# The down projection of a two-layer encoder in plain and block groups, with outputs added onto the residual in DRAM

## The chip, the cores and the metric

The kernel runs on one core of a Trainium2 chip. The core has five engines with instruction streams of their own: TensorE (PE, matrix products into PSUM, with weight loads, PEld, running beside them), VectorE (DVE), ScalarE (ACT), GpSimd (POOL) and SyncE (SP), and 16 DMA engines behind queues. Here SP's queue carries the loads and POOL's queue the stores. The metric is the time on the device in microseconds (us); a smaller one is better.

## The reference, cut to what matters

The model has two layers over 1040 columns (16 learned meta columns and 1024 frames) of width 1024. The change concerns the second half of a layer, `conv_ffn`:

```python
def conv_ffn(x, w_up, conv_w, conv_b, w_down):
    h = x @ w_up
    ...
    u, g = jnp.split(hc, 2, axis=-1)
    return (jax.nn.silu(g) * u) @ w_down
...
for i in range(DEPTH):
    ...
    h = h + jnp.concatenate([o_gla, o_fox], axis=-1) @ w_out[i]
    h = h + conv_ffn(rms_norm(h, ffn_norm[i]), w_up[i], conv_w[i], conv_b[i], w_down[i])
return rms_norm(h, final_norm)[:, N_META:]
```

All is in fp32. The gated width is 2816 = 22 tiles of 128, the output width 8 tiles of 128. The last `@ w_down`, with the addition onto h, is the down projection.

## The kernel before, in words

Activations lie transposed: a tile is 128 features on the partitions by up to 1040 columns. A product of fp32 numbers is made from three matmuls (`mm3`, lines 217 to 219): each operand is split into a rounded part `hi` and a rest `lo`, and hi*hi, lo*hi and hi*lo are added in PSUM. A split is a copy on ScalarE (the cast to `hi`) and a subtraction on VectorE (`lo`): lines 184 and 186 for plain weights, 1019 and 1020 for weights of blocks, 331 and 332 for activations.

A layer runs through attention, the output projection, the up projection, and the down projection. During the output projection the residual h goes to DRAM (`hm`, line 1102, stores on POOL's queue). The up projection (`ffn_up`) works on 2 x 2 blocks: of a pair of output tiles (u and g), two halves of the inner dimension and two halves of the columns, seven block products are made instead of eight, on sums and differences of the blocks (weights: lines 980 to 1021, with `S1 = A21 + A22` made by an accumulating DMA for the first few tiles at line 996; results: copies out of PSUM by ScalarE at line 1189, additions by VectorE at 1188). Each of the 22 gated tiles is stored to DRAM (`actd`).

The down projection is the product of 22 gated tiles with a weight for 8 output tiles. `load_act` loads a gated tile from `actd` on SP's queue and splits it. `FGROUPS` cuts the 22 tiles into groups of 5, 5, 5, 4 and 3. For each of the first four groups and each output tile m, `dense3` runs the matmuls of the group over column chunks, 400, 384 and 256 wide in layer 0 and 512 and 512 in layer 1 (where the meta columns are no longer needed), with the weights of the next output tile loaded ahead (`stream`, line 205); VectorE adds the PSUM result onto h[m] on chip (line 1259), h having been loaded from `hm` as the stage begins (line 1373). The PSUM pool of this stage has eight banks of 512 numbers. The last group, tiles 19 to 21, is computed by `down_last` chunk by chunk over all eight outputs, and feeds the next layer's norm or the final one.

The order of the instructions on TensorE is that of the program text (`manual_schedule`); on VectorE, ScalarE, POOL and SP a scheduler sets the order when the kernel is built, and a queue keeps its order from then on: an instruction that waits holds up all behind it on its queue. Tiles live in a pool of equal slots on chip (`Slots`, 33 of them, with some added by stage); `get` takes a free slot, and a writer of a reused slot waits for the readers of what was there, DMAs among them.

The three central lines of the accumulation before:

```python
def ev(ps, c0, n):
    h = hT[m][:, c0:c0 + n]
    nc.vector.tensor_tensor(out=h, in0=ps, in1=h, op=ALU.add)
```

## Time and profile before

| What | Number |
|---|---|
| Median of 3 runs | 2629.63 us (2625.71 to 2631.41) |
| The profiled execution, its own time | 2631.03 us |
| Its span | 2629.3 us |
| TensorE busy | 2526.3 us, 96% of the span |
| VectorE busy | 1751.8 us, 67% |
| ScalarE busy | 1241.9 us, 47% |
| GpSimd busy | 402.9 us, 15% |
| Layer 0, groups 5, 5, 5, 4 of the down projection | 1062.30 to 1279.97 us |
| Layer 1, the same | 2365.49 to 2577.00 us |

How to read the profile's rows: a busy time is followed by its number of instructions (x...). In a row of a table by windows the columns are the window, its length, the busy time of each engine, then the clock granted to TensorE (1.00 is full), the DMA engines' busy share and GB/s. A row of a group of instructions has line, engine, operation, out<-in with shapes and count; behind the bar the busy time in us and the mean of one in ns; behind the second bar the idle time of the engine just before them and what ended it. A row with a time in front is a single instruction: start, duration, engine, line, and in brackets the idle time before it. A row of DMAs has the size of one and the median us from issue to landing.

### The profile page before, as it was taken

Reading aid. Unit: us, or ns where it says so; the run is one execution under the profiler, and the core shown is the slowest. Engines: PE = TensorE matmul, PEld = TensorE weight load, DVE = VectorE, ACT = ScalarE, POOL = GpSimd, SP = SyncE. Lnnn points to the kernel's source line nnn. Section 1 sums busy time; section 2 is a strip of 40 time slices with the busy share of each in tenths; the row PEclk is TensorE's granted clock in tenths of the full one; section 3 lists DMA queues with packets and bytes.
Section 4 is the critical chain, followed back from the end, with each engine's and each line's share of the span. In section 5 each row is a group of like instructions: output and inputs, shape, how many; then the busy total and the mean of one; then the engine's idle time right before and its main releaser. Section 6 shows DMA issues by size and latency. Waiting matters only on the chain.

```text
span 2629.3 us, 46309 instructions
## 1 busy us (share of the span) xinstructions
PE 2526.3 (96%) x18102; PEld 2407.3 (92%) x18102; DVE 1751.8 (67%) x3514; ACT 1241.9 (47%) x2677; POOL 402.9 (15%) x566
## 2 busy tenths in 40 slices
PE   8999999899999999999999999998999999999997
PEld 7988898898999999999999888888899999998886
DVE  7655766759877777643665665666698677776335
ACT  6345665635544445321443565665464444453112
POOL 4033333310000000000201333332100000000002
PEclk9999999999999999999999999999999999999999
DMA  3222123342322223522311222142523222245222
GB/s 124 67 83 71 44 86 122 105 145 89 105 77 83 80 81 100 209 90 59 106 52 66 75 73 74 56 133 92 164 73 113 79 79 74 84 154 179 62 57 75
DMA packets 117355, 245.96 MB, mean 94 GB/s; under 512 B 14752, under 2 KB 36512, under 8 KB 117136
## 3 DMA queue, kind: packets, MB, share of 16 engines
q1 hardware_dynamic: 97440, 184.89, 22.4%
q0 software_dynamic: 17824, 55.80, 6.2%
q8 instruction: 142, 2.33, 0.3%
q10 hardware_dynamic: 1872, 2.31, 0.2%
q14 instruction: 77, 0.63, 0.1%
HBM read 179.26 MB, written 50.91 MB: 88 GB/s over the span
## 4 chain that ended last, share of the span: by engine, by line
PE 76%; DVE 12%; issue 4%; ACT 4%; DMA 2%; POOL 1%; SPq 0%; DVEq 0%; POOLq 0%; ACTq 0%
PE mm L217 12%; PE mm L218 12%; PE mm L219 12%; PE up L217 9%; PE up L219 9%; PE up L218 9%; PE av L707 2%; PE tr L689 2%; DVE S L656 2%; PE wo L217 1%; PE wo L218 1%; PE wo L219 1%; DVE PT L332 1%; DVE x L1044 1%; DMA cb<-cd 1%
## 5 line engine op out<-in xcount | busy, mean ns | idle before, releaser
L217 PE MATMUL up<-x,hi 128*128 128x260 f32 (+1 forms) x2464 | 698.9, 284 | 2.3 <-ACT x L1043 1.6
L219 PE MATMUL up<-x,hi 128*128 128x260 f32 (+1 forms) x2464 | 697.8, 283 | 1.9 <-DVE x L1044 1.8
L218 PE MATMUL up<-x,lo 128*128 128x260 f32 (+1 forms) x2464 | 697.5, 283 | 0.8 <-DVE lo L1020 0.8
L219 PEld LDWEIGHTS up<-x,hi 128*128 128x128 f32 x2464 | 466.5, 189 | 2.9 <-DVE x L1044 2.9
L217 PEld LDWEIGHTS up<-x,hi 128*128 128x128 f32 x2464 | 465.9, 189 | 3.5 <-ACT x L1043 2.2
L218 PEld LDWEIGHTS up<-x,lo 128*128 128x128 f32 x2464 | 466.3, 189 | 1.0 <-DVE lo L1020 1.0
L217 PE MATMUL mm<-xh,hi 128*128 128x348 f32 (+4 forms) x1056 | 365.2, 346 | 0.0
L218 PE MATMUL mm<-xh,lo 128*128 128x348 f32 (+4 forms) x1056 | 340.9, 323 | 0.0
L219 PE MATMUL mm<-xl,hi 128*128 128x348 f32 (+4 forms) x1056 | 340.7, 323 | 0.0
L1020 DVE TENSOR_TENSOR lo<-raw,hi 128x512 fp32r<-128x512 f32 x308 | 210.1, 686 | 140.2 <-ACT hi L1019 140.2
L184 ACT CAST hi<-raw 128x512 fp32r<-128x512 f32 (+1 forms) x264 | 143.1, 544 | 334.0 <-PE mm L219 238.1
L218 PE MATMUL mm<-ah,lo 128*128 128x400 f32 (+1 forms) x760 | 266.5, 351 | 0.9 <-DVE lo L186 0.9
L219 PE MATMUL mm<-al,hi 128*128 128x400 f32 (+1 forms) x760 | 265.4, 349 | 0.0
L217 PE MATMUL mm<-ah,hi 128*128 128x400 f32 (+1 forms) x760 | 265.4, 349 | 0.0
L1019 ACT CAST hi<-raw 128x512 fp32r<-128x512 f32 x308 | 190.3, 621 | 113.8 <-PE up L219 87.2
L186 DVE TENSOR_TENSOR lo<-raw,hi 128x512 fp32r<-128x512 f32 (+1 forms) x196 | 110.8, 569 | 175.3 <-ACT hi L184 171.6
L217 PEld LDWEIGHTS mm<-xh,hi 128*128 128x128 f32 x1056 | 201.0, 190 | 6.0 <-issue 5.3
L218 PEld LDWEIGHTS mm<-xh,lo 128*128 128x128 f32 x1056 | 200.9, 190 | 0.4 <-issue 0.3
L219 PEld LDWEIGHTS mm<-xl,hi 128*128 128x128 f32 x1056 | 199.8, 189 | 0.4 <-issue 0.3
L668 ACT ACTIVATE P<-S,m 116x460 f32<-116x460 f32 (+2 forms) x224 | 125.1, 562 | 76.2 <-DVE m L656 72.1
L332 DVE TENSOR_TENSOR PT<-tr,PT 116x464 fp32r<-116x464 f32 (+3 forms) x240 | 122.1, 516 | 57.5 <-ACT PT L331 55.9
L218 PEld LDWEIGHTS mm<-ah,lo 128*128 128x128 f32 x760 | 142.8, 188 | 14.6 <-DVE lo L186 1.5
(248 smaller groups left out, 5106.5 us busy)
## 6 DMA issues: line engine op xcount, KB each, us to landing
raw<-in_wm_dram SPq DMA_DIRECT2D x338, 256.0 KB, 2.7
raw<-in_wd_dram SPq DMA_DIRECT2D x64, 256.0 KB, 2.7
actd<-cv POOLq DMA_DIRECT2D x22, 520.0 KB, 3.0
st<-actd SPq DMA_DIRECT2D x22, 520.0 KB, 4.6
actd<-cv POOLq DMA_DIRECT2D x22, 512.0 KB, 2.9
st<-actd SPq DMA_DIRECT2D x22, 512.0 KB, 4.9
cb<-cd SPq DMA_DIRECT2D x16, 520.0 KB, 4.2
kA<-kA SPq DMA_DIRECT2D x24, 260.0 KB, 3.8
```

Of the source, the lines that this page charges most:

```text
L184: nc.scalar.copy(hi[:, :n, :], raw[:, :n, :])
L186: eng.tensor_tensor(out=lo[:, :n, :], in0=raw[:, :n, :], in1=hi[:, :n, :].bitcast(F32), op=ALU.subtract)
L217: nc.tensor.matmul(ps, wh, xh[:, c0:c0 + n], start=first, stop=False, skip_group_check=more)
L218: nc.tensor.matmul(ps, wl, xh[:, c0:c0 + n], start=False, stop=False, skip_group_check=more)
L219: nc.tensor.matmul(ps, wh, xl[:, c0:c0 + n], start=False, stop=last, skip_group_check=more)
L332: nc.vector.tensor_tensor(out=lo, in0=src, in1=hi.bitcast(F32), op=ALU.subtract)
L656: nc.vector.tensor_tensor_reduce(out=S[:rows, :n], in0=S[:rows, :n], in1=cb[:rows, c0:k1], scale=1.0, scalar=(BIG if ci == 0 else m[:rows, ...
L668: nc.scalar.activation(P[:rows, :n], S[:rows, :n], AF.Exp, scale=-1.0, bias=m[:rows, nch - 1:nch], accum_out=(den if nch == 1 else d3[:row ...
L689: nc.tensor.transpose(tr[:w, j, :rows], P[:rows, o:o + w], id_)
L707: nc.tensor.matmul(av[:, a:width], w.rearrange("p a b -> p (a b)"), x, start=(t == 0 and i == 0), stop=(t == last and i == 1))
L1019: nc.scalar.copy(hi[:], src[:])
L1020: nc.vector.tensor_tensor(out=lo[:], in0=src[:], in1=hi[:].bitcast(F32), op=ALU.subtract)
```

## The change

The 19 tiles that were in groups of 5, 5, 5 and 4 are now in four groups of two kinds: 3 plain tiles, 8 tiles in blocks, 4 plain tiles, 4 tiles in blocks. The last group of 3 stays with `down_last`.

In a plain group ("n") the matmuls run over the two column halves, each a double bank of PSUM filled by two matmuls per product (260 wide in layer 0; 256 in layer 1, `HALVES_OUT`). ScalarE copies the result into one of three rotating tiles `do`, and POOL issues an accumulating DMA of the whole tile onto `hm[m]` in DRAM. In a block group ("s", `down_blocks`) a pair of output tiles is computed from seven block products, as in the up projection: the blocks are the two outputs, the two halves of the group's tiles and the two column halves. The products of a pair run in the order 1, 2, 6, 5, 7, 4, 3, with product 1 of the next pair between 7 and 4 for pairs 1 and 2, and for pair 0 between 2 and 6. Products 1, 6, 7 and 4 share one double bank, each adding to what is there, and ScalarE copies its state after each of them; 2 and (5, 3) have banks of their own, added by VectorE. Each finished output goes to `hm` by an accumulating DMA, except the last pair of the last block group: there VectorE adds it onto h7 and h6, loaded on chip by then. h0 to h5 are loaded after the block group, ahead of `down_last`.

The operands of the block groups (sums and differences of halves of gated tiles, and their splits) are made by a generator, `prepare`, which `pump` advances as slots come free, from the last products of the up projection on. The down stage now runs in the PSUM pool of the up projection (four double banks). `block_operand` and `up_split` are the old `up_operand` and `up_split` with the number of inner tiles as an argument.

The diff, cut to its core:

```diff
-CH_DOWN = [(16, 512), (528, 512)]
-FGROUPS = [(0, 5), (5, 5), (10, 5), (15, 4), (19, 3)]
-HALVES, HALVES_LAST = (0, 520, 520), (8, 524, 516)
+GROUPS, LAST = (("n", 0, 3), ("s", 3, 8), ("n", 11, 4), ("s", 15, 4)), (19, 3)
+HALVES, HALVES_LAST, HALVES_OUT = (0, 520, 520), (8, 524, 516), (16, 528, 512)
...
+    def prepare(self, halves, acts, X):
...
+        for kind, g0, ng in GROUPS + (("r",) + LAST,):
...
+            if kind != "s":
+                for j in range(g0, g0 + ng):
+                    yield 2 + size()
+                    fetch()
+                    t = use()
+                    ah, al = s.get(F32R, "ah"), s.get(F32R, "al")
+                    self.split(ah[:, own], al[:, own], t[:, own])
+                    s.put(t)
+                    acts[j] = (ah, al)
+                continue
...
+                a0, a1, b0, b1 = use()
+                put(1, a0)
+                yield m
+                put(2, b0)
+                yield 1 + m
+                tt(a1, b1, a1, ALU.subtract)
+                t2 = get("t2")
+                tt(t2, a1, a0, ALU.add)
+                put(6, t2)
+                yield m
+                tt(a0, b1, t2, ALU.subtract)
+                put(5, a0)
...
+                put(7, a1)
...
+                tt(b0, b0, t2, ALU.subtract)
...
+                put(4, b0)
...
+                put(3, b1)
...
+    def pump(self, n, keep=0):
+        s = self.slots
+        while n and self.need + keep <= len([i for i in s.free if i not in s.lent]):
+            self.need = next(self.prep)
+            n -= 1
+
+    def down_blocks(self, lyr, g0, ng, X, pp, fw, halves, after, residual=None):
...
+        NP = KD // 2
+        seq = [(0, 1), (0, 2), (1, 1), (0, 6), (0, 5), (0, 7), (0, 4), (0, 3)]
+        for j in range(1, NP):
+            seq += [(j, 2), (j, 6), (j, 5), (j, 7)] + ([(j + 1, 1)] if j + 1 < NP else []) + [(j, 4), (j, 3)]
...
+        def out(j, m, t):
+            if residual and j == NP - 1:
+                h = residual(m)[:, o0:T]
+                nc.vector.tensor_tensor(out=h, in0=t[:, o0:T], in1=h, op=ALU.add)
+            else:
+                nc.gpsimd.dma_start(self.hm[m][:, o0:T], t[:, o0:T], accum_op=ALU.add)
+            s.put(t)
+
+        def evacuate(j, p):
+            q = st[j]
+            add = lambda out, ps: nc.vector.tensor_tensor(out=two(out), in0=ps[:, :, :n], in1=two(out), op=ALU.add)
+            copy = lambda out: nc.scalar.copy(two(out), q["a"][:, :, :n])
+            if p == 1:
+                q["u"] = s.get(F32, "du")
+                copy(q["u"][:, t0])
+            elif p == 2:
+                add(q["u"][:, t0], q["y"])
+            elif p == 6:
+                copy(q["u"][:, t1])
+            elif p == 7:
+                q["g"] = s.get(F32, "dg")
+                copy(q["g"][:, t1])
+                add(q["g"][:, t1], q["x"])
+            elif p == 4:
+                copy(q["g"][:, t0])
+                out(j, 2 * j + 1, q["g"])
+            elif p == 3:
+                add(q["u"][:, t1], q["x"])
+                out(j, 2 * j, q["u"])
...
+    def ffn_down(self, lyr, pp, fw, halves, acts, X, ids):
...
+        def plain(kind, g0, ng, m, w, nxt):
...
+            out = hT[m] if kind == "r" else going[m % 3]
+            for h in range(2):
+                ps = pp.tile([128, 2, 512], F32, tag=f"p{(2 * m + h) % 4}", name="down", bufs=1)
+                for k in range(ng):
+                    for c in range(2):
+                        self.mm3(ps[:, c, :n], w[k], acts[g0 + k], halves[h] + c * n, n, k == 0, k == ng - 1)
+                x = two(out[:, halves[h]:halves[h] + W])
...
+                    nc.scalar.copy(x, ps[:, :, :n])
+            if kind == "n":
+                nc.gpsimd.dma_start(self.hm[m][:, o0:T], out[:, o0:T], accum_op=ALU.add)
...
-                    self.ffn_up(lyr, mix, hT, pp, fw, HALVES_LAST if last else HALVES, o0, during_last)
+                    tail, down = self.ffn_down(lyr, pp, fw, halves, acts, X, ids)
+                    self.ffn_up(lyr, mix, hT, pp, fw, HALVES_LAST if last else HALVES, o0, tail)
+                    hT = down()
...
-                    hT = [s.get(F32, f"h{k}", first=ids) for k in range(KD)]
-                    for k in range(KD):
-                        nc.sync.dma_start(hT[k][:, o0:T], self.hm[k][:, o0:T])
...
-                    self.stream(self.down_tiles(lyr, hT, pp, o0, CH_DOWN if last else CH, acts))
                     nm = self.down_last(lyr, hT, pp, dch, acts, at_end, ids)
```

226 lines of the change are left out of this document (185 added, 41 removed).

## The prediction

> **What bounds the kernel now.** First the page's busy times and the chain of work that ended last.
>
> ```profile
> PE 2526.3 (96%) x18102; PEld 2407.3 (92%) x18102; DVE 1751.8 (67%) x3514; ACT 1241.9 (47%) x2677; POOL 402.9 (15%) x566
> ...
> PE 76%; DVE 12%; issue 4%; ACT 4%; DMA 2%; POOL 1%; SPq 0%; DVEq 0%; POOLq 0%; ACTq 0%
> ```
>
> TensorE is busy for 96% of the span and is 76% of the chain. The change touches the down projection only, so that stage is read alone: first in layer 0, then in layer 1, from the first matmul of a down weight to the first of the last three tiles, and behind them layer 0's last three tiles.
>
> ```profile
> 1062.30:1279.97 217.67, 216.73 (x1371) 216.45 (x1370) 99.49 (x182) 49.38 (x82) 0.53 (x1) 1.00 0.32 102
> 2365.49:2577.00 211.51, 211.51 (x914) 171.31 (x913) 96.59 (x147) 48.15 (x80) 0.53 (x1) 1.00 0.31 98
> 1279.97:1346.36 66.39, 66.39 (x418) 65.05 (x417) 44.86 (x79) 34.82 (x71) 22.76 (x25) 1.00 0.28 98
> ...
> 1063.66 0.45 PE L218 MATMUL mm<-ah,lo 128*128 128x400 f32 x1 [0.94 <-DVE lo L186]
> ```
>
> The columns are length, PE, PE weight load, DVE, ACT, POOL, granted clock, DMA share, GB/s. TensorE is busy all the time but for one stall of 0.94 us, at full clock; VectorE works for under half of the stage, ScalarE for a quarter, and 0.32 of the DMA time is used. So the stage lasts as long as its matmuls, and anything that makes TensorE wait is added in full.
>
> **The matmuls.** Nineteen tiles by eight outputs by three chunks by three products are 1368 matmuls in layer 0, and 912 with two chunks of 512 in layer 1. After the change a column half of 520 or 512 is two matmuls of 260 or 256. Plain groups: 7 tiles x 8 x 4 x 3 = 672. The 8 tiles in blocks: 4 pairs x 7 products x 4 x 2 x 3 = 672 (768 if plain). The 4 in blocks: 336 (384 if plain). Together 1680 a layer. What one takes, from the up projection (width 260, then 258) and from two starts 42 matmuls apart (width 256):
>
> ```profile
> 700.00:800.00 100.00, 100.00 (x838) 100.00 (x837) 10.43 (x15) 11.89 (x20) 1.00 0.23 80
> 2100.00:2200.00 100.00, 100.00 (x834) 100.00 (x833) 10.36 (x15) 11.78 (x20) 1.00 0.23 80
> ...
> 1341.04 0.28 PE L217 MATMUL mm<-xh,wl 128*128 128x256 f32 x1
> 1346.01 0.28 PE L217 MATMUL mm<-xh,wl 128*128 128x256 f32 x1
> ```
>
> Width 260 takes 100/838 = 0.1193 us, width 256 takes 4.97/42 = 0.1183. Layer 0: 1680 x 0.1193 = 200.5 against 217.67, a gain of 17.2. Layer 1: 1680 x 0.1183 = 198.8 against 211.51, a gain of 12.7. Gross gain 29.9 us. The rest is what TensorE will wait for.
>
> **Prices of the added work.**
>
> ```profile
> L1189 ACT COPY hg<-up 128x520 f32<-128x520 f32 x44 | 26.1, 594 | 71.0 <-PE up L219 71.0
> L1188 DVE TENSOR_TENSOR hu<-up,hu 128x520 f32<-128x520 f32 x44 | 30.5, 693 | 0.0
> L332 DVE TENSOR_TENSOR al<-st,ah 128x1040 fp32r<-128x1040 f32 x22 | 27.2, 1239 | 22.9 <-ACT ah L331 16.2 <-DMA actd<-cv 3.8 <-issue 2.9
> L331 ACT CAST ah<-st 128x1040 fp32r<-128x1040 f32 x22 | 23.4, 1064 | 28.3 <-DMA st<-actd 25.0 <-DVE al L332 3.4
> L1002 DVE TENSOR_TENSOR raw<-raw,raw 128x512 f32<-128x512 f32 x166 | 107.9, 685 | 1.3 <-DMA raw<-in_wm_dram 1.2
> L1020 DVE TENSOR_TENSOR lo<-raw,hi 128x512 fp32r<-128x512 f32 x308 | 210.1, 686 | 140.2 <-ACT hi L1019 140.2
> L186 DVE TENSOR_TENSOR wl<-raw,wl 128x384 fp32r<-128x384 f32 x16 | 8.8, 557 | 18.2 <-ACT wl L184 18.0 <-PE mm L219 0.2
> ...
> 1042.15 0.28 PE L219 MATMUL up<-x,hi 128*128 128x260 f32 x1
> 1042.54 0.59 ACT L1189 COPY hg<-up 128x520 f32<-128x520 f32 x1
> ```
>
> VectorE per layer (all 1040-wide operand work at 1.24, weights of the group of 4 at half the 512-wide time): 31 splits and 12 sums of operands 53.3; 28 weight splits and 16 weight sums in each block group 30.2 + 15.1; 16 plain weight splits 9.9; 24 additions from PSUM 16.6; two additions onto h 2.5: 127.6 us in a stage of 200. ScalarE takes 64 copies (38.0) and 31 casts (33.0) beside the casts of weights. Both have cover on the mean; waits arise at places:
>
> (a) *A product that follows its predecessor in the same bank.* In pair 0 and in pair 3 of each block group, product 4 stands right behind product 7 and goes on in its bank, so it waits until ScalarE has copied product 7 out. The last two rows give it: the copy starts 0.39 us after the start of the last matmul it needs (0.28 of matmul, 0.11 of lag), takes 0.59, and the release back costs about 0.11; instead of 0.12 the next start is 1.09 later: 0.97, call it 1.0. Eight such places: 8.0 us. If ScalarE is in a 1.06 us cast then, half of that more at some; if the copy is released before the drain, 0.6. Range 4.8 to 9.6.
>
> (b) *From the second plain group to the group of 4.* Three output tiles rotate and go to DRAM by an accumulating DMA on POOL's queue. In the built program the cast of the last activation tile sits on ScalarE ahead of the last copy out of PSUM and waits for the accumulation of output 6 (its buffer); the split behind it on VectorE waits for that of output 7, ahead of the addition that product 3 of pair 0 needs. An output takes TensorE 48 x 0.119 = 5.7 us, so output 6's accumulation has about that before it delays anybody. Before has 520 KB stores and 256 KB accumulating loads only:
>
> ```profile
> actd<-cv POOLq DMA_DIRECT2D x22, 520.0 KB, 3.0
> ...
> raw<-in_wm_dram POOLq DMA_DIRECT2D x10, 256.0 KB, 4.2
> raw<-in_wm_dram SPq DMA_DIRECT2D x338, 256.0 KB, 2.7
> ...
> q0 software_dynamic: 144, 0.26, 25.9%
> ...
> q0 software_dynamic: 144, 0.53, 21.4%
> ```
>
> The first three are KB and median us to landing. The last two are the queue's packets, MB and share of 16 engines: 25.9% of 7 us = 1.8 us for an accumulation of 0.26 MB, 21.4% of 6 us = 1.28 us for a store of 0.53 MB. Landing time L of a 520 KB accumulation: at least the store plus the 1.5 us that accumulation adds at 256 KB (4.2 - 2.7), 4.5; at most twice the small one, 8.4. I take 5.5, nearest to the store: its 3.0 us plus twice 1.8 minus 1.28 gives 5.3, and some queueing. Then the wait is the cast of 1.06 plus 0.1: 1.2 a layer, 2.4 together. Each further us of L costs one per layer, and from 6.8 on the second wait costs another: 8.4 gives 11.4 in all, a landing within 4.5 gives 0.
>
> The Trainium skill (page "DMA: Bandwidth & Descriptors", section "Anatomy of one DMA — SWDGE (gpsimd) path") fits 2.0 us plus bytes/436e3 us for a DMA from GpSimd, an estimate of 3.2 us here, by which (b) and (c) would be nothing and the sum 2.8 lower; the store's 3.0 agrees with it, the accumulation's 4.2 against 2.6 does not, so I do not take it.
>
> (c) *Inside the group of 8*, the cast for the second plain group waits for output 4's accumulation, ahead of the copy that product 4 of pair 3 needs: 0.4 together at L = 5.5, up to 5.
>
> (d) *From the group of 4 to the last three tiles.* The last product (12 matmuls, 1.43 us) starts as product 4 ends; behind that end VectorE has lag and copy (0.70), the addition onto h7 (1.24), the addition of product 3 (0.69), the low part of the first weight (0.56) and lag: 3.4, less 1.43 and one matmul: 1.9 a layer, 3.8. It is 2.4 if the scheduler's weight work slips ahead, 6 if h7 is late. Loads of h move here from the stage's start; they and the last raw weights queue on SP behind the load of h4, which waits for that accumulation, with about 3 us to spare at L = 6: nothing, and beyond that part of the 6.
>
> (e) *The first plain group* lasts 3 x 8 x 12 x 0.1193 = 34.4 us, in which VectorE must do ten 1040-wide splits, five sums and the weights, 29 to 32 us. It nearly fits: 0.5 a layer, 0 to 2; together 1.0. DMA is closer still there, eight accumulations beside the loads. It has run full before, at the same place:
>
> ```profile
> 1066.00:1068.00 2.00, 2.00 (x15) 2.00 (x14) 2.00 (x4) 0.91 (x2) 0.00 (x0) 1.00 1.04 424
> ```
>
> (f) *Products of half the length.* In the group of 4 a product is 1.43 us and a copy with its lags 0.81; whenever ScalarE is in a cast of 1.06 the copy is late by up to 0.4. 1 a layer, 2 together, 0 to 4.
>
> (g) *Clock.* Where TensorE idled 2 of 5 us, the next 5 us ran at 0.51, 26 matmuls instead of 44:
>
> ```profile
> 650.00:655.00 5.00, 2.99 (x13) 2.08 (x12) 5.00 (x9) 3.89 (x7) 0.00 (x0) 0.80 0.20 59
> 655.00:660.00 5.00, 5.00 (x26) 5.00 (x25) 3.45 (x6) 0.00 (x0) 0.89 (x1) 0.51 0.39 93
> 660.00:665.00 5.00, 5.00 (x44) 5.00 (x43) 4.01 (x6) 3.96 (x5) 0.00 (x0) 1.00 0.22 61
> ```
>
> That is 18/44 of 5 us, 2.0 lost. The end of the group of 4 has 1.0 of (a) and 1.9 of (d) within some 6 us: an even chance, 1 a layer, 2.0 together, 0 to 4.
>
> The Trainium skill (page "TensorE: Matmul & The Clock Gate", section "HAM oscillation — how this bites in real kernels") wants an idle gap of over about 3.4 us before the clock drops; by that (g) is nothing and the sum 2.0 lower. The rows show the drop after 2.0 us of idling within 5, so (g) stays.
>
> Sum of (a) to (g): 8.0 + 2.4 + 0.4 + 3.8 + 1.0 + 2.0 + 2.0 = 19.6; net -29.9 + 19.6 = -10.3. Lower ends: 4.8 + 2.4 = 7.2, net -22.7. Upper ends: 9.6 + 11.4 + 5 + 6 + 4 + 4 + 4 = 44, net +14. The last three tiles and the final norm, unchanged, cost what they cost.
>
> The profiled execution took 2631.03 us, 1.4 above the median of 2629.63 (2625.71 to 2631.41): 2631.0 - 10.3 = 2620.7, and 2619.3 against the median; I say 2620.
>
> **The rivals.**
>
> *Slower: accumulations land late.* At L = 8.4, (b) costs 9.0 more, (c) 4.6, (e) 3.0: net +6.3, about 2636, and 2644 with all the upper ends. It starts to decide at L about 7.5, where the net is nothing. For it: accumulation takes 1.8/0.26 against 1.28/0.53, nearly three times the packet time per byte, and the 7.8 us that the loads of h needed below, when many 520 KB transfers came together. Against: outputs come 4.3 to 10 us apart, not at once.
>
> ```profile
> h<-hm SPq DMA_DIRECT2D x8, 520.0 KB, 7.8
> ```
>
> *No change worth the name.* Joints and clock at their upper ends, (a) 9.6, (d) 6, (f) 4, (g) 4 with (b), (c), (e) as above: 27.4, net -2.5, 2627. For it: after each joint TensorE has only 12 matmuls to hide a copy in. Against: the up projection, with the same copies, ran 838 matmuls in 100 us with no wait.
>
> *A gain twice as large.* Landings within 4.5 us, no clock loss, preparation hidden: net -22.7, 2607. For it: 127.6 us of VectorE in 200. The skill's formula for a DMA from GpSimd would give this.
>
> *Operands are late.* If what VectorE prepares in the first plain group (e) is not done when the group of 8 begins, TensorE stands until it is. At 5 us a layer, three operand splits and a sum, the price is 10, 9 above (e): net -1; at 9 us it is slower by 7, 2636. The estimate of 29 to 32 in 34.4 speaks against it, a DMA share of 1.04 for it.
>
> **How the numbers follow.** Forecast (-5 to -17) 0.43; gain twice as large 0.14; nearly no change 0.15; late landings 0.20; late operands and slower 0.08. A measurement of this kernel tells a change of 0.2%, 5.3 us, from none. Faster 0.57, same 0.15, slower 0.28. Range: 2607, the lower ends, to 2644, the upper ends, since the slower cases hold more than 2 in 10; the forecast's own range is 2613 to 2625.
>
> **What would show it.** Layer 0's stage 200.5 us of matmuls and about 10 of waits, layer 1's the same within 2; eight gaps of about 1.0 ahead of product 4, ended by ScalarE; a gap of about 1.2 at the first products of the group of 4 ended by ScalarE; a gap near 2 ahead of the last three tiles ended by VectorE, and perhaps a granted clock near 0.5 behind it; landings of the accumulations near 5.5 us. A landing above 7.5, or a gap of several us ahead of the first block product, makes the prediction wrong.

## The result and the profile after

The changed kernel takes 2636.86 us (median of 20 runs), the kernel before 2630.36 (20 runs): ratio 1.0027, 95% interval [1.0018, 1.0035]. It is slower by 0.3%, 6.5 us; one of its 20 runs, at 2743.13 us and a granted clock of 0.85, is left out of the ratio. The time lies inside the predicted range, but the forecast was a gain of 10 us. The profiled execution took 2643.37 us, span 2641.6, 6.5 us above the median; between the two stretches compared below, attention and the up projection of layer 1 took 1031.6 us in it (1344.60 to 2376.20) against 1027.1 before (1338.39 to 2365.49), though hardly any of their code changed. The profiles of the runs below have 1024.9 to 1037.7 there. So the comparison goes by stage.

The page of the changed kernel, busy times and chain:

```profile
PE 2513.2 (95%) x19182; PEld 2432.2 (92%) x19182; DVE 1803.2 (68%) x3544; ACT 1337.8 (51%) x2855; POOL 454.3 (17%) x626
...
PE 72%; DVE 14%; ACT 5%; DMA 4%; issue 3%; POOL 1%; SPq 0%; DVEq 0%; ACTq 0%; POOLq 0%
```

TensorE is busy for 13 us less than before, yet the span is longer: its share of the chain fell from 76% to 72%, and ScalarE's and the DMAs' rose from 6% to 9% together. By windows of the changed kernel: the stage of layer 0, its last three tiles up to the first transpose of layer 1, the stage of layer 1, and the rest:

```profile
1064.45:1277.68 213.23, 204.82 (x1683) 203.15 (x1681) 115.97 (x166) 96.81 (x164) 26.51 (x31) 0.99 0.71 159
1277.68:1344.60 66.92, 61.97 (x351) 59.50 (x349) 47.96 (x82) 33.37 (x72) 22.86 (x25) 0.95 0.45 149
2376.20:2587.41 211.21, 202.40 (x1682) 200.76 (x1681) 114.91 (x166) 96.12 (x164) 26.50 (x31) 0.99 0.71 159
2587.41:2641.60 54.19, 39.46 (x232) 34.23 (x230) 37.53 (x72) 17.96 (x39) 17.44 (x16) 0.90 0.35 127
```

The kernel before, for the second and fourth of them:

```profile
1279.97:1338.39 58.42, 58.42 (x351) 57.08 (x350) 40.71 (x71) 30.45 (x63) 22.76 (x25) 1.00 0.29 103
2577.00:2629.30 52.30, 39.00 (x231) 33.90 (x229) 31.80 (x63) 15.43 (x32) 17.38 (x16) 0.90 0.23 81
```

Against the windows shown in the prediction, the stages gain 4.4 us (217.67 to 213.23) and 0.3 (211.51 to 211.21); what follows them loses 8.5 (58.42 to 66.92) and 1.9 (52.30 to 54.19). The sum, +5.7 us, agrees with the medians' 6.5.

What TensorE waited for, in layer 0 (from 1064.4 to 1345) and in layer 1 (from 2376.2 on); total us, times, longest:

```profile
PE down L218 <- ACT dg L1380: 4.7, 4, 2.7
PE mm L218 <- ACT wl L185: 3.3, 1, 3.3
PE mm L219 <- DVE wl L187: 1.6, 2, 1.4
PE down L218 <- ACT do L1468: 1.3, 1, 1.3
PE down L218 <- ACT du L1380: 1.3, 1, 1.3
...
PE down L218 <- ACT dg L1380: 4.6, 4, 2.6
PE down L218 <- ACT do L1468: 2.7, 1, 2.7
PE mm L219 <- DVE wl L187: 1.4, 1, 1.4
```

Most of it stands behind a copy or a cast on ScalarE, an engine that is busy for under half of these stages (96.81 of 213.23).

**Where the 8.5 us go.** Single instructions of the changed kernel, on ScalarE, VectorE and SP, around the end of layer 0's blocks:

```profile
1276.93 1.75 ACT L185 CAST wl<-raw 128x384 fp32r<-128x384 f32 x4
1284.60 0.51 ACT L185 CAST wl<-raw 128x384 fp32r<-128x384 f32 x1 [5.92 <-DMA raw<-in_wd_dram]
1285.02 0.63 ACT L293 ACTIVATE xh<-h,vec 128x400 fp32r<-128x400 f32 x1
...
1278.83 0.55 DVE L187 TENSOR_TENSOR wl<-raw,wl 128x384 fp32r<-128x384 f32 x1
...
1277.72 1.27 SPq L1439 DMA_DIRECT2D h<-hm  x3
1279.41 0.33 SPq L179 DMA_DIRECT2D raw<-in_wd_dram  x1
```

Four of the eight weights of the last three tiles are cast; the fifth has not been loaded, because its buffer is the first one's and VectorE frees it only at 1279.38, behind the addition onto h7. Three loads of h, 520 KB each, have just been issued, the DMA engines are full (below), and the weight is cast 5.2 us after its issue. ScalarE stands for 5.92 us, and the first cast of the norm's input for layer 1 (`xh`), queued behind, starts at 1285.02: 7.3 us after the first matmul of these tiles, where before it was 2.5 (1282.43 against 1279.97). The norm's feed passes from VectorE to ScalarE and back for every output, has the splits of four more weights in it and does not catch up. Among its last casts on ScalarE stands the cast of a weight of layer 1 that TensorE comes to next. It starts 41.7 us behind the first matmul of the last three tiles; before, the same cast started 35.4 us behind it (1315.41). TensorE waits 3.34 us for this cast and then runs at half clock:

```profile
1319.39 0.60 ACT L185 CAST wl<-raw 128x512 fp32r<-128x512 f32 x1
1320.05 0.70 PE L218 MATMUL mm<-xh,wl 128*128 128x400 f32 x1 [3.34 <-ACT wl L185]
...
1320.00:1323.40 3.40, 3.15 (x8) 2.72 (x9) 3.37 (x6) 2.90 (x7) 1.29 (x3) 0.50 0.47 133
1323.40:1326.80 3.40, 3.40 (x13) 3.38 (x13) 2.56 (x5) 1.27 (x3) 2.23 (x5) 0.57 0.74 203
```

21 matmuls in 6.8 us; before, the window from 1319 to 1323 had 24 in 4.0, so some 3.3 us are lost here. With the wait of 3.34 and the 1.4 ahead of the second matmul of the stretch, that is 8.0 of the 8.5. The DMA share around this point, changed kernel first, then the kernel before:

```profile
1275.00:1280.00 5.00, 3.59 (x28) 3.31 (x27) 3.31 (x5) 2.24 (x5) 0.00 (x0) 1.00 0.94 290
1280.00:1285.00 5.00, 5.00 (x30) 4.95 (x29) 2.42 (x5) 0.40 (x1) 0.00 (x0) 1.00 1.00 375
```

```profile
1275.00:1280.00 5.00, 5.00 (x35) 5.00 (x34) 2.52 (x7) 0.41 (x1) 0.00 (x0) 1.00 0.54 161
1280.00:1285.00 5.00, 5.00 (x30) 5.00 (x29) 2.49 (x6) 1.80 (x4) 0.00 (x0) 1.00 0.29 103
```

**Where the stages' gain went.** The longest gap, 2.67 us ahead of product 4 of the last pair in layer 0's group of 8 (1179.64). ScalarE of the changed kernel ahead of it:

```profile
1172.24 1.06 ACT L332 CAST ah<-st 128x1040 fp32r<-128x1040 f32 x1 [4.75 <-DMA hm<-du]
1173.20 0.58 ACT L1380 COPY du<-down 128x520 f32<-128x520 f32 x1
...
1175.76 1.06 ACT L332 CAST x<-t 128x1040 fp32r<-128x1040 f32 x1 [1.45 <-DVE t L1310]
1177.08 2.02 ACT L332 CAST x<-st 128x1040 fp32r<-128x1040 f32 x2 [0.26 <-DVE st L1310]
1179.00 0.58 ACT L1380 COPY dg<-down 128x520 f32<-128x520 f32 x1
```

A cast for the next plain group waits 4.75 us until the accumulation that reads the buffer it reuses has landed; the copy of `du` behind it is late by 1.26. Then three casts for the next block group, which wait for sums on VectorE, stand ahead of the copy of `dg`. The landings, us (minimum, median, maximum), of the accumulations from blocks (L1374) and from plain groups (L1470):

```profile
DMA to landing us min/median/max: 5.3/6.8/9.3
...
DMA to landing us min/median/max: 5.3/5.8/8.8
```

### The profile page after: what moved, and what is told of

Its sections match the earlier page's. It is cut to its first block, busy times and chain, and to the rows that moved or that the text cites. A ratio compares the mean times of both kernels' runs of the same rounds, so it can differ in the third digit from the quotient of the medians.

```text
span 2641.6 us, 48860 instructions
## 1 busy us (share of the span) xinstructions
PE 2513.2 (95%) x19182; PEld 2432.2 (92%) x19182; DVE 1803.2 (68%) x3544; ACT 1337.8 (51%) x2855; POOL 454.3 (17%) x626
## 3 DMA queue, kind: packets, MB, share of 16 engines
q0 software_dynamic: 26464, 87.51, 13.3%
## 4 chain that ended last, share of the span: by engine, by line
PE 72%; DVE 14%; ACT 5%; DMA 4%; issue 3%; POOL 1%; SPq 0%; DVEq 0%; ACTq 0%; POOLq 0%
PE up L218 9%; PE up L219 9%; PE up L220 9%; PE mm L218 6%; PE mm L219 6%; PE mm L220 6%; PE down L218 4%; PE down L219 4%; PE down L220 4%; PE av L708 2%; PE tr L690 2%; DVE S L657 2%; PE wo L219 1%; PE wo L218 1%; PE wo L220 1%
## 5 line engine op out<-in xcount | busy, mean ns | idle before, releaser
L1024 DVE TENSOR_TENSOR lo<-raw,hi 128x512 fp32r<-128x512 f32 (+1 forms) x420 | 272.1, 653 | 228.9 <-ACT hi L1023 225.9
L1023 ACT CAST hi<-raw 128x512 fp32r<-128x512 f32 (+1 forms) x420 | 246.8, 592 | 161.4 <-PE up L220 88.0
L218 PE MATMUL down<-x,hi 128*128 128x260 f32 (+1 forms) x672 | 192.1, 286 | 16.5 <-ACT dg L1380 9.4
L219 PE MATMUL down<-x,lo 128*128 128x260 f32 (+1 forms) x672 | 190.7, 284 | 0.0
L220 PE MATMUL down<-x,hi 128*128 128x260 f32 (+1 forms) x672 | 190.6, 284 | 0.0
L1006 DVE TENSOR_TENSOR raw<-raw,raw 128x512 f32<-128x512 f32 (+1 forms) x230 | 142.8, 652 | 41.9 <-DMA raw<-in_wd_dram 37.5
L1217 POOL DMA_DIRECT2D actd<-cv x44 | 23.6, 536 | 764.8 <-DVE cv L1216 743.8
L690 PE MATMUL tr<-ident,P 116*116 116x116 f32 x704 | 129.5, 272 | 24.0 <-DVE PT L333 23.9
```

The costliest lines, as they stand in the source:

```text
L218: nc.tensor.matmul(ps, wh, xh[:, c0:c0 + n], start=first, stop=False, skip_group_check=more)
L219: nc.tensor.matmul(ps, wl, xh[:, c0:c0 + n], start=False, stop=False, skip_group_check=more)
L220: nc.tensor.matmul(ps, wh, xl[:, c0:c0 + n], start=False, stop=last, skip_group_check=more)
L690: nc.tensor.transpose(tr[:w, j, :rows], P[:rows, o:o + w], id_)
L1006: nc.vector.tensor_tensor(out=q[out][:, :nk, :], in0=q[a][:, :nk, :], in1=q[b][:, :nk, :], op=op)
L1023: nc.scalar.copy(hi[:, :nk, :], src[:, :nk, :])
```

## The experiments

Ratios are to the kernel before, run on the same chip beside each. The stage lengths are those of each kernel's profile, cut at the same instructions: the first down matmul, the first matmul of the last three tiles (in the joint column up to the first transpose of layer 1). The medians come from more than one chip, so a difference between two runs is better taken from their ratios. A profile is one execution: that of e14 took 8.7 us more than its median, that of e17 5.9 more and that of e12 7.2 less, so a stage is compared with a stage and not with a total.

| Run | Median us | Ratio [95%] | Stage layer 0 | Joint | Stage layer 1 |
|---|---|---|---|---|---|
| before | 2630.36 | | 217.67 | 58.42 | 211.51 |
| changed | 2636.86 | 1.0027 [1.0018, 1.0035] | 213.23 | 66.92 | 211.21 |
| e2_own_raw | 2648.03 | 1.0066 [1.0045, 1.0086] | 220.80 | 62.61 | 219.57 |
| e3_order | 2624.83 | 0.9984 [0.9973, 0.9994] | 209.26 | 66.53 | 206.13 |
| e4_plain_stores | 2625.37 | 0.9991 [0.9978, 1.0004] | 209.29 | 63.98 | 205.86 |
| e5_late_casts | 2627.98 | 1.0005 [0.9994, 1.0016] | 212.01 | 65.33 | 210.95 |
| e6_order_late_casts | 2622.07 | 0.9980 [0.9969, 0.9992] | 206.44 | 62.66 | 207.99 |
| e9_all_plain | 2664.90 | 1.0146 [1.0126, 1.0165] | 224.36 | 63.05 | 223.59 |
| e10_no_onchip_add | 2641.91 | 1.0058 [1.0039, 1.0076] | 211.62 | 68.06 | 213.27 |
| e14_held | 2628.00 | 0.9999 [0.9986, 1.0012] | 207.10 | 69.14 | 204.62 |
| e12_order_casts_held | 2625.28 | 0.9979 [0.9965, 0.9993] | 205.38 | 68.00 | 203.20 |
| e13_order_casts_adds | 2625.59 | 0.9988 [0.9975, 1.0000] | 204.90 | 68.24 | 202.36 |
| e17_order_held_early_casts | 2619.70 | 0.9970 [0.9958, 0.9981] | 206.75 | 70.01 | 202.23 |
| e16_blocks8_last | 2625.93 | 0.9995 [0.9984, 1.0005] | 209.62 | 62.32 | 213.07 |

### The order of the products

```diff
-        seq = [(0, 1), (0, 2), (1, 1), (0, 6), (0, 5), (0, 7), (0, 4), (0, 3)]
+        seq = [(0, 1), (0, 2), (0, 6), (1, 1), (0, 7), (0, 5), (0, 4), (0, 3)]
-            seq += [(j, 2), (j, 6), (j, 5), (j, 7)] + ([(j + 1, 1)] if j + 1 < NP else []) + [(j, 4), (j, 3)]
+            seq += [(j, 6), (j, 2), (j, 7), (j, 5)] + ([(j + 1, 1)] if j + 1 < NP else []) + [(j, 4), (j, 3)]
...
                 copy(q["g"][:, t1])
+            elif p == 5:
                 add(q["g"][:, t1], q["x"])
```

> The order of the block products alone is changed: 6, 2, 7, 5, (1 of the next pair), 4, 3, and for pair 0: 1, 2, 6, 1 of pair 1, 7, 5, 4, 3. No product follows its predecessor in a bank any more; the addition of product 5 comes behind 5. Theory A, the gaps ahead of product 4 are the copy of product 7 by ScalarE: the eight gaps of 0.68 to 2.7 us ended by the copy of dg (9.4 us together) fall under 1 us together, and with them the half clock behind the two of 2.7: total 8 to 11 us shorter, about 2627. Rival B, ScalarE itself is late there, held by a cast that waits for an accumulating DMA: the six gaps of 0.68 go (4 us), the two of 2.7 stay near 2 at another product: total 4 us shorter, about 2633.

Measured 2624.83 us, 12 under the changed kernel's median (11 by the two ratios), and faster than the kernel before. The six bare joints are gone, and so are the two long ones at that place. Of the long ones a part came back elsewhere: 1.78 us ended by the copy of `du`, 1.68 by an addition on VectorE. The two stages are 4.0 and 5.1 us shorter:

```profile
1058.43:1267.69 209.26, 204.08 (x1682) 203.04 (x1681) 116.39 (x166) 96.75 (x164) 26.50 (x31) 0.99 0.72 166
1267.69:1334.22 66.53, 61.64 (x351) 59.21 (x349) 47.92 (x82) 33.51 (x72) 22.98 (x25) 0.95 0.44 147
2368.39:2574.52 206.13, 200.83 (x1682) 199.79 (x1681) 114.92 (x166) 96.14 (x164) 26.50 (x31) 0.99 0.74 167
```

So the joints cost what theory A says, about 0.84 us each beyond a matmul; the waits from preparation (B) are a second cause beside them. The joint to layer 1 did not move (66.53).

### The landing of the accumulations

```diff
-                nc.gpsimd.dma_start(self.hm[m][:, o0:T], t[:, o0:T], accum_op=ALU.add)
+                nc.gpsimd.dma_start(self.hm[m][:, o0:T], t[:, o0:T])
...
-                nc.gpsimd.dma_start(self.hm[m][:, o0:T], out[:, o0:T], accum_op=ALU.add)
+                nc.gpsimd.dma_start(self.hm[m][:, o0:T], out[:, o0:T])
```

> The transfers of finished outputs onto hm are plain stores instead of accumulating ones (the sum over the groups and with the residual is left out, all else is the same). Theory A, casts and splits that reuse a tile wait for the accumulation to land (8.1 + 14.5 us of ScalarE and 4.3 + 3.9 us of VectorE in the changed kernel): landing falls from 5.8 and 6.8 to about 3.5 us, those waits to a quarter, the gaps of TensorE of 1.26 to 2.71 us ended by ScalarE's copies (10.7 us, six of them) fall to about 0.7 each or nothing: total 6 to 9 us shorter with the half clock behind the longest. For the fifth raw weight of the last three tiles: if it is the load of h4 ahead of it on SP's queue that delays it, it is issued some 3 us earlier against the end of the blocks; if it is the raw buffer that VectorE frees, it is issued at the same place, about 1.7 us behind the first matmul of the last three tiles, and only lands sooner. Rival B, the casts are late because their inputs are: the gaps stay as they are, total within 2 us.

Measured 2625.37 us, 11.5 under the changed kernel (9.5 by the two ratios). The gaps at the first products of the group of 4 (1.32 and 0.76 us in layer 0, 2.71 and 0.42 in layer 1) are gone, and so are those ahead of product 7 in the group of 8 (1.26 and 0.64); the long one at product 4 stays, 2.65 us in layer 0 and 2.44 in layer 1. So the first ones hang on the landing, and the last does not. What stands ahead of it, the casts in ScalarE's queue, is tried by e14 below. For the fifth weight: it is issued 1.73 us behind the first matmul of the last three tiles (1269.91), exactly as in the changed kernel (1279.41 against 1277.68), and is cast after a stand of 3.64 us instead of 5.92.

```profile
1271.64 0.33 SPq L179 DMA_DIRECT2D raw<-in_wd_dram  x1
...
1274.56 0.51 ACT L185 CAST wl<-raw 128x384 fp32r<-128x384 f32 x1 [3.64 <-DMA raw<-in_wd_dram]
```

So the raw buffer that VectorE frees sets the issue, not the load of h4 ahead of it on SP's queue. The transfer takes less: the last three loads of h, which wait for accumulations to land, are issued 3.0 to 5.9 us ahead of it here and 0.8 to 1.7 us in the changed kernel.

### The casts in ScalarE's queue

```diff
+    def held(self):
+        return self.tc.issue_after(self.copied.ins) if self.copied else nullcontext()
     def pump(self, n, keep=0):
...
-            self.need = next(self.prep)
+            with self.held():
+                self.need = next(self.prep)
```

(`copied` is the last copy out of PSUM that the program made; `issue_after` keeps what follows behind it on its engine.)

> The changed kernel with one difference: on ScalarE the casts of the operands prepared ahead stand behind the copy out of PSUM that the program made last before them (in the changed kernel the scheduler had put them ahead of it). No transfer, no buffer and no order on TensorE differs. Theory A, it is the place of these casts on ScalarE that makes its copies late (the gaps of 1.26 and 2.67 us at products 7 and 4 of pair 3 of the group of 8, of 1.32 and 2.71 at the first products of the group of 4, and their like in layer 1; plain stores left the 2.67 as it was): those gaps fall to the 0.7 of the bare copy or below, 8 us of TensorE together with the half clock, total 6 to 9 us shorter than the changed kernel's 2636.9. Rival B, the operands then come late for the next group: the gaps move to its first matmuls, ended by VectorE's splits, total within 3 us of the changed kernel.

2628.00 us, 8.9 under the changed kernel (7.4 by the two ratios). Both stages lose 6 us and more (213.23 to 207.10, 211.21 to 204.62), the block products of layer 0 show only the bare joints of 0.68 us and one of 1.02:

```profile
1068.40:1275.50 207.10, 202.69 (x1683) 201.44 (x1681) 115.61 (x167) 97.66 (x165) 26.51 (x31) 1.00 0.74 163
1275.50:1344.64 69.14, 63.04 (x350) 59.42 (x349) 48.03 (x82) 33.59 (x72) 22.89 (x25) 0.95 0.44 146
2376.10:2580.72 204.62, 200.32 (x1682) 199.10 (x1681) 115.17 (x167) 97.02 (x165) 26.49 (x31) 1.00 0.73 163
```

Theory A holds: the same work, later in the queue, costs the stages nothing. The waits at the first products of the group of 4 that ScalarE's copy ended are gone too, so a late landing reaches TensorE there by way of a cast that stands ahead of a copy; those that VectorE's addition ended stay (1.02 and 0.56 us). But the joint grew by 2.2 us. On SP's queue the load of the fourth weight of the last three tiles now stands behind four of the loads of h and is issued 2.3 us behind the first matmul (1277.76); in the changed kernel it stands ahead of five of them (1269.33). ScalarE has only three weights to cast ahead of the feed and stands 6.05 us for the fourth.

### The joint of the last three tiles with layer 1

First, buffers of their own for the weights of outputs 4 to 7:

```diff
+                if m >= KD // 2:
+                    own = s.get(F32, "wr", (128, 2, 4, 128), es)
...
+            raw = own[:, m % 2, :ng, :]
+            nc.sync.dma_start(raw, self.wd[lyr, m][:, g0:g0 + ng, :])
```

> Only the raw weights of outputs 4 to 7 of the last three tiles get a buffer of their own (before: the four raw buffers shared with the weights of the blocks), so that they are loaded ahead of the residual h. In the changed kernel ScalarE stood 5.92 us for the fifth of them (cast at 1284.60), the norm feed of the next layer queued behind it began at 1285.02, and TensorE stood 3.34 us at 1320.05 and ran at half clock until 1326.8. Theory A, this wait of ScalarE sets the start of layer 1: the idle of 5.9 us is gone, the feed begins about 3 us earlier, the stand at the start of layer 1 and its half clock go, and the stretch from the first matmul of the last three tiles to the first transpose of layer 1 falls from 66.9 to about 60.5 us: total 6 us shorter, about 2631. Rival B, the alternation of VectorE and ScalarE in the feed (about 1.5 us an output) is the bound once TensorE comes sooner, whatever the weights: that stretch stays at 65 or more, total within 2 us of the changed kernel.

The joint fell by 4.3 us (66.92 to 62.61) and ran at full clock, but the two tiles taken for it shifted the reuse of all others: new waits of 2.3 to 3.3 us in the group of 4, stages longer by 7.6 and 8.4, total 2648. And ScalarE stood as long as before, 6.46 us, now for a weight of layer 1 (cast at 1285.53), so the idle of theory A is not gone. The feed begins 7.8 us behind the first matmul, later than in the changed kernel (7.3), and yet the cast that TensorE waits for at the start of layer 1 comes 1.8 us sooner (39.9 us behind it instead of 41.7). So the start of the feed alone does not set the joint; its pace does too, and here the splits of four weights are out of it. The second run takes no tile:

```diff
+                if c0 == dchunks[0][0] and 0 < m <= KD // 2:
+                    with self.tc.issue_after(self.fed.ins):
+                        w[m + 3] = self.weights(self.wd[lyr, m + 3][:, g0:g0 + ng, :], w[m + 3])
```

> The weights of outputs 4 to 7 of the last three tiles are loaded and split as in the changed kernel, but their casts stand on ScalarE behind the norm feed of outputs 1 to 4 instead of ahead of output 0's. No tile is added. Theory A, ScalarE's wait for a load (5.92 us) ahead of the feed sets the start of layer 1: the first cast of the feed moves from 7.3 us behind the first matmul of the last three tiles to about 5, the stand of 3.34 us at the start of layer 1 to about 1, its half clock goes: the stretch from the first matmul of the last three tiles to the first transpose falls from 66.9 to 61 to 63, total 4 to 6 us shorter, about 2632. Rival B, the feed is late from its inputs (the loads of h, which fill the DMA engines here) or from its own pace: 65 or more, total within 2 us.

The feed begins at 4.8 us and the wait at the start of layer 1 is gone, as theory A has it, and so is its half clock; but the weights now come late for TensorE inside the last three tiles (0.5, 0.4, 0.5 and 1.0 us), the feed is held up on its way (3.00 us for a weight of layer 1), and the joint is 65.33, 1.6 shorter only, the 65 or more of rival B. The total fell by 8.9 us (5.8 by the two ratios), more than the profile's stretches explain (1.7 in both layers together); that part stays open.

> The order of the block products of e3_order and the late casts of e5_late_casts together. If the two losses are separate, they add: e3_order's 2624.8 less 4 to 6, about 2620, faster than the kernel before by 0.3 to 0.4%. If TensorE's gain in the stage is eaten by the feed of the norm, which starts no earlier, 2624 to 2626.

2622.07, faster than the kernel before by 0.2%. That is between the two alternatives: 2.8 us under e3_order by the medians, 1.1 by the two ratios, whose intervals overlap. By the profiles the joint is 3.9 shorter (66.53 to 62.66) and the stage of layer 1 is 1.9 longer.

### The blocks and the addition on chip

`GROUPS` as 5, 5, 5 and 4 plain tiles:

> Groups of 5, 5, 5 and 4 plain tiles as before the change, but with the copies by ScalarE, the accumulating transfers onto hm, the two column halves and the late loads of h of the change. 1824 matmuls a layer instead of 1680: 217.6 and 215.8 us. Theory A, the plain groups cost no waits and the whole gain of the change is the products that the blocks save: the stages of layer 0 and 1 last 218 to 220 and 216 to 218 us, and what follows them is as late as in the changed kernel (66.9 and 54.2 us): total 2643 to 2648. Rival B, the accumulating transfers cost waits in plain groups too: stages of 223 or more, total over 2652.

2664.90, 28 us over the changed kernel, as B has it. The stages are 224.36 and 223.59 us against 217.6 and 215.8 of bare matmuls, with waits of up to 2.2 and 2.5 us where ScalarE's copy or VectorE's split is late. B's reason, the accumulating transfers, is not shown: ahead of the copy that ends the 2.2 us, ScalarE's casts wait 2.61 us for the load of a weight. The blocks are what pays in the change: 11 to 12 us a layer by the stages. Plain groups with everything else of the change are worse than the kernel before's.

And `None` in the place of `residual`, so that the last pair goes to `hm` as well:

> The last block pair goes to hm by accumulating transfers like the others, and h6 and h7 are loaded behind it; nothing else is changed. Theory A, the two additions of 1.24 us on VectorE are what TensorE waits for ahead of the last three tiles (1.41 and 1.35 us): that wait falls under 0.7, and the price moves to h6 and h7, which arrive about 11 us behind the last product (landing 6.8, load 4.3) where output 6 needs them 10 us behind it: stretch from the last three tiles to the first transpose 66 to 69, total within 3 us of the changed kernel. Rival B, the wait is the weights' own: it stays at 1.4.

Neither: the wait falls from 1.41 to 1.08 us and from 1.35 to 1.02, and new ones of 3.70 and 3.08 us stand later in the last three tiles, ended by the cast of a weight; in layer 0 ScalarE stands 6.78 us for its load. Without the addition onto h7 TensorE still waits for VectorE to add product 3 (1269.61, as that product ends) and to split the first weight behind it. 2641.91, 5 us over the changed kernel (8 by the two ratios): the addition on chip is worth its place.

### All together

e12 has the order of e3, the late casts of e5, the held casts of e14, prepares nothing for the group of 4 in the last pair of the group of 8, and takes no operand tile as the last plain output ends. e13 adds the last pair onto h7 and h6 behind the first four weights. e17 is e12 without the late casts.

> e6_order_late_casts with the casts held as in e14_held, no operands of the group of 4 prepared in pair 3 of the group of 8, and none taken from the tiles of the last plain output as soon as it ends. If the losses are separate: gaps of the two stages, 4.7 and 8.2 us in e6_order_late_casts, fall to about 2 each, total 2622 less 8: 2614 to 2617. If VectorE's and ScalarE's work only moves, 2620 to 2624.

> e12_order_casts_held, and VectorE adds the last pair onto h7 and h6 behind the splits of the first four weights of the last three tiles instead of ahead of them. Theory A, the wait of 1.4 us ahead of the last three tiles in both layers is VectorE's addition of 1.24 us onto h7: it falls to 0.3 or less, total 2 us under e12_order_casts_held. Rival B, the price moves into the feed of layer 0's last three tiles: total equal within 1 us.

> e12_order_casts_held without its late casts: the eight weights of the last three tiles are cast ahead of the norm feed as in the changed kernel. Its stages should stay at 205 and 203 us. Theory A, from the last three tiles on the end of layer 0 is set by what must land there (the last accumulating transfers, the loads of h behind them, the weights behind these on SP's queue), so that a shorter stage gives a longer joint: stretch from the first matmul of the last three tiles to the first transpose 68 to 71 us, more than the 66.9 of the changed kernel with its stage of 213, total 2624 to 2628. Rival B, the late casts made e12's 68.0: 62 to 65, total 2619 to 2622.

In e12 the gaps of the stages are down to 2.6 and 4.6 us, and the stages at 205.38 and 203.20, against 200.5 and 198.8 of matmuls; but the joint is 68.00. The total, 2625.28, is not under e6's. SP's queue of e12 shows a likely reason: as in e14, the fourth weight (the first of the five in the second row) stands behind four loads of h.

```profile
1257.35 9.84 SPq L1446 DMA_DIRECT2D h<-hm  x4
1267.29 6.03 SPq L179 DMA_DIRECT2D raw<-in_wd_dram  x5
```

e13 moves 0.35 us of the 1.4 (to 1.07 and 1.02) and wins nothing: B. e17 has the stages that were expected and theory A's long joint, 70.01:

```profile
1061.74:1268.49 206.75, 203.33 (x1682) 202.91 (x1681) 116.51 (x167) 96.50 (x165) 26.50 (x31) 0.99 0.74 167
1268.49:1338.50 70.01, 62.40 (x351) 59.34 (x350) 48.04 (x82) 33.69 (x72) 22.75 (x25) 0.95 0.42 142
...
1276.56 1.16 ACT L185 CAST wl<-raw 128x384 fp32r<-128x384 f32 x2 [7.47 <-DMA raw<-in_wd_dram]
```

ScalarE stands 7.47 us for the fourth weight, which SP issues at 1272.01, right behind loads of h that waited for an accumulation to land. That is theory A's path. A shorter stage as such need not lengthen the joint: e3, also with early casts, has a stage 4.0 us shorter than the changed kernel's and a joint no longer (66.53). e12, e13, e14 and e17 have the fourth weight behind the loads of h and joints of 68.0 to 70.0; the changed kernel and e2 to e6 have it ahead and joints of 62.6 to 66.9. No run changes this order alone, so that it is the cause is not shown. The total of e17 is rival B's: its median, 2619.70, is the lowest of all and beats the kernel before by 0.3% ([0.9958, 0.9981]) and the changed kernel by 0.6%; its interval overlaps those of e3, e6, e12 and e13, so that the order among these is not settled.

```diff
-GROUPS, LAST = (("n", 0, 3), ("s", 3, 8), ("n", 11, 4), ("s", 15, 4)), (19, 3)
+GROUPS, LAST = (("n", 0, 4), ("s", 4, 4), ("n", 8, 3), ("s", 11, 8)), (19, 3)
```

> e12_order_casts_held with the groups 4 plain, 4 in blocks, 3 plain, 8 in blocks, 3 plain, the same 1680 matmuls. The last pairs are now those of the group of 8, whose products take 2.86 us instead of 1.43: the last accumulating transfer is issued about 20 us ahead of the last product instead of 10. Theory A, landings, loads of h and weights crowd the DMA engines at the end of layer 0 (share 0.94 to 1.00 for 15 us in the changed kernel, 0.3 to 0.5 before): the crowd is gone ahead of the last three tiles, the stretch from there to the first transpose falls from 68.0 to 60 to 62, total 5 to 7 us under e12_order_casts_held, about 2619, unless the operands of the group of 8 are late at its start. Rival B, they are late, since they must be made beside a plain group of 34 us: a gap of several us ahead of the first block product, ended by ScalarE or VectorE, total 2630 or more.

Both theories show in the stretches. With the long products last, the joint falls from 68.00 to 62.32 us and runs at full clock:

```profile
1267.71:1330.03 62.32, 59.63 (x350) 56.79 (x349) 48.15 (x81) 32.60 (x69) 23.65 (x25) 1.00 0.39 129
2356.09:2569.16 213.07, 202.29 (x1683) 201.06 (x1681) 118.10 (x169) 98.50 (x169) 26.48 (x31) 0.98 0.72 171
```

But the operands of the group of 8 are late: gaps of 4.95 us in layer 0, 3.43 and 4.73 in layer 1, ended by VectorE near its first products, and stages of 209.62 and 213.07. The total, 2625.93, does not move. Nor is it shown that the earlier landings shorten the joint: e6, with the short products last, has 62.66. What both have and e12 lacks is the fourth weight issued ahead of the last loads of h (1255.60 in e16).

## Why the prediction was wrong

Its mechanism of the gain was right: 1680 matmuls a layer at the rates taken; where the waits were cleared the stages came to 205 and 202 us beside the 200.5 and 198.8 of the sum. Several terms came out near: (a) eight joints at 0.84 us, 6.7 together, where 1.0 each was said (at two of them a longer wait lay on top, counted under (c)); (d) 1.6 and 1.5 us ahead of the last three tiles (1.9 said); (e) 1.1 together (1.0 said). (f) did not occur: 0 where 2.0 was said.

From the forecast's net of -10.3 to the +5.7 of the four stretches it is 16.0 us. Two terms that were mis-sized, (b) and (c), make 9.2 of them, and what follows the stages, beyond (d), 7.3. The rest nearly cancels: (a), (d) and (f) were 4.0 lower than said, the clock in the stages 0.7 higher, and 2.7 stay open.

**The step that failed** in what follows the stages is in (d): "Loads of h move here from the stage's start; they and the last raw weights queue on SP behind the load of h4 … nothing, and beyond that part of the 6", with the sentence that the last three tiles "cost what they cost". They cost 8.5 us more in layer 0, of which 1.6 is (d): 6.9 us that no term held. The text looked at one queue for a wait of TensorE. What it missed is that ScalarE waits too: the norm's feed, which sets the start of layer 1, is queued behind a weight whose buffer is freed late and whose transfer shares full DMA engines with the loads of h, and it has further weights to split on its way. The cast that the start of layer 1 hangs on came 41.7 us behind the first matmul of the last three tiles instead of 35.4. e4 showed the buffer and the loads of h, e2 and e5 that the start of the feed alone does not decide. How the 6.9 us divide among the late weights, their order on SP and the splits in the feed stays open, since no run changes one of them alone.

**Two terms were mis-sized.** (c), "0.4 together", was 6.1 us: 1.42 and 0.79 ahead of product 7, by a cast that waits for a landing as (c) has it, and 2.0 and 1.9 beyond the bare joint ahead of product 4, in the last pair of the group of 8. Its rule, one wait at a landing of 5.5, left out the three casts of operands behind it in ScalarE's queue; e4, with its sooner landings, kept the wait that these make, and e14, which puts them behind the copy, took it away. (b), "2.4 together", was 5.9 (1.5 and 0.9, 2.9 and 0.6). The rule for its first wait held: from the issue of output 6's accumulation to the cast that reuses its buffer it was 5.9 us in layer 0 (1228.26 to 1234.16) and 7.3 in layer 1 (2537.61 to 2544.88), not 5.5, and with these the rule gives 1.6 and 3.0. The second wait came already at 6.3 and 5.9 us, where the text had it from 6.8 on. e4 took both waits away.

(g) was 2.0 "at the end of the group of 4"; the clock fell elsewhere, where the waits were long: in the window from 1179.60 on 15 matmuls ran in 3.4 us at 0.50 (28 fit), 1.6 us lost; from 2489.40 on 19 at 0.63, 1.1 lost; and behind the wait at layer 1's start. That (g) comes near in the stages is luck.

The rival "accumulations land late" named the slower side and gave +6.3, near the measured 6.5, in part for its reason. The median landings were 5.8 and 6.8, below its 7.5, and the waits that hang on a landing, those of (b) and the ones ahead of product 7, came to 8.1 us where 2.8 was said; the rest of the loss is the casts in the queue and the joint. That the two sums meet is luck. The rule of the Trainium skill (page "DMA: Bandwidth & Descriptors", section "Anatomy of one DMA — SWDGE (gpsimd) path") that would have made (b) and (c) nothing gives an estimate of 3.2 us for these transfers; the shortest landing here is 5.3, so the runs decide against it for accumulating transfers. By itself it would have moved the sum by 2.8 us, and not to the 22.7 of the rival "a gain twice as large".

## What to carry to other kernels

What a change moves to the end of a stage comes due in the next one: list the instructions that the next stage's first result hangs on, on every engine, and ask of each whether its buffer, its load and its place in the queue still come in time. An engine that is half idle still delays the one that bounds, if work prepared ahead stands in its queue before the copy that is wanted; holding such work behind the copy cost a few lines and gave 7 to 9 us. And where a product adds onto a bank that must first be copied out, put another product between.

## What the runs showed of the hardware

An accumulating transfer of 512 or 520 KB into DRAM takes the DMA engines about twice as long as a plain one. The software queue's share rose from 6.2% of 2629.3 us before to 13.3% of 2641.6 with the 60 accumulating transfers, and to 9.6% of 2619.4 in e4, where the same 60 are plain: 188 and 88 us more, or 3.1 and 1.5 us of all 16 engines each. The changed kernel and e4:

```profile
q0 software_dynamic: 26464, 87.51, 13.3%
q0 software_dynamic: 26464, 87.51, 9.6%
```

POOL issues an accumulating one in 0.86 us, a plain one in 0.54. The clock can fall behind a wait of 2.6 to 2.7 us, and not always: the same wait in layer 1 left it at 0.63 over the 3.4 us that stood at 0.50 in layer 0, and the wait of 2.71 us at 2546.46 did not slow the matmul behind it (0.38 us, where the one at 1179.64 took 0.58). In e12 it fell behind a wait of 1.92 us with no other that the profile shows in the 15 us before: 15 matmuls in the 3.4 us from 1232.60 on, at 0.50.

```profile
1179.60:1183.00 3.40, 3.36 (x15) 3.36 (x16) 3.22 (x4) 0.00 (x0) 0.00 (x0) 0.50 0.03 10
2489.40:2492.80 3.40, 3.38 (x19) 3.38 (x20) 3.15 (x4) 0.00 (x0) 0.00 (x0) 0.63 0.08 20
```

The Trainium skill (page "TensorE: Matmul & The Clock Gate", section "What's actually happening") tells of a window of about 3.4 us that runs freely. That a wait of the same length shows in one place and not in another would agree with it, but no run here moves a wait against such a window. The idle time that the section asks for, about 3.4 us, is more than the 1.92 that sufficed here.
